# Seven right and nine left expert buffers, row transposes placed behind the up products, mixr beside mixc, and 128-byte operand starts in the second block

## The chip, the cores and the metric

The kernel runs on one core of one Trainium2 chip. Its time is the device time of one execution in microseconds (us); a smaller number is better. Before the change three executions took 3399.05, 3403.66 and 3410.57 us, median 3403.66 us.

## The reference

The kernel computes two transformer-like blocks on 512 tokens of width 2048, all in float32.

The first block normalises x, projects it with w_in, and runs two mixers on the projection: a gated depthwise convolution (31 taps) and a linear-attention scan over 16 heads of 64. Their outputs, 1024 wide each, are joined and go through w_out:

```python
    mixed = jnp.concatenate([y_conv, y_rwkv], axis=-1)
    h = h + mixed @ w_out[l]
    v = rms_norm(h, norm_ffn[l])
    h = h + hierarchical_moe(v, router_group_w[l], ...)
    return rms_norm(h, norm_final)
```

The mixture of experts picks one group of eight by four group logits, then two of that group's eight experts by 32 expert logits; each expert is `silu(x @ w_gate) * (x @ w_up) @ w_down` with a hidden width of 512. There are 32 experts, and all their weights (three matrices of 4 MB each) are read.

The second block normalises, projects to eight parts, and runs sliding-window attention (16 heads of 64 in 4 key groups, window 128) and a diagonal complex state-space recurrence (64 groups, 64 states) side by side:

```python
    q, k, v, a_gate, u, z, g_a, g_s = split(h @ w_in)
    y_a = (attention(q, k, v, sinks) * silu(a_gate)) @ w_attn_proj
    y_ssm = gelu(s5_ssm(u, ...))
    glu_a, glu_b = split(y_ssm @ w_glu + b_glu)
    y_s = (glu_a * sigmoid(glu_b) * silu(z)) @ w_ssm_proj
    merged = sigmoid(g_a) * y_a + sigmoid(g_s) * y_s
    x = x + merged @ w_out
```

## The kernel before, in words

The program has three stages, one after the other in the span: phase A (the first block up to w_out, to about 1017 us), phase B (routing and the experts, to about 2030 us) and phase C (the second block, to the end). A scheduler in the framework orders the instructions of each engine by its own model of their times; a `with tc.issue_after(ins)` block asks that what is issued in it stands behind `ins`. Engines run their instructions in order. Tiles live in pools, on the left or the right side of the on-chip memory; a pool that is closed gives its addresses to the next one, and an instruction that writes there waits for the last reader of the old tile.

**Dense products.** A product in float32 is split into three (`mm3`, L110 to 113): each operand x is held as a rounded part `xh` and a rest `xl`, and the sum is `ah@bh + ah@bl + al@bh`. In the phase C layout the moving operand of a product is an activation tile (128 x 512) and the stationary one a 128 x 128 piece of weights; in w_out of phase A it is the other way round, with weights moving. `weights` (L99) loads a piece by SyncE's queue into `wraw`, ScalarE rounds it (`wh`, L47), VectorE forms the rest (`wl`, L48; GpSimd in w_out(0)). The activations are `uh`/`ul` in phase A, `u2h`/`u2l` for the 16 x 128-row normalised input of the second block, `ge` (the state-space output), `ys` (the gated one), `att` (attention) and `mg` (the merged one).

**w_out in two halves.** `w_out(0)` (L250) multiplies the convolution output `mixc`, `w_out(1)` the scan output `mixr`. `mixr` and the row tiles `xr` come from a right-side pool `mixr`, opened when the pools before it are closed. Behind each quarter of columns of `w_out(1)`, `routed` (L699) transposes the new rows (L708), copies them to `hT` (L711, L713), and adds their part to the router logits: for the first three quarters by four products of 36 x 512 (L717), turned round at the end of the third (L725), for the last by 16 products of 128 x 36 (L731). The rows are also written to memory (`dTok`, L274).

**Experts.** The experts run in 16 pairs, and each pair takes 24 loads of 1 MB on SyncE's queue (L672): gate and up for four quarters of the inner dimension, then down for four quarters of the columns, for both experts. The loads go round 16 buffers, `NW[0]` in the right pool `expw` and `NW[1]` in the left pool `expw2`; the down loads of the last pair go left in any case. Up to `NW[0]` loads are issued during w_out(1) (L258), the next `NW[1]` when the left pool is there. For the rows of a pair there is a gather by an indirect transfer on GpSimd's queue into one tile `xg` (L787), which is set to zero once before (L764); `turned` (L804) transposes `xg` on TensorE (L811). `main` (L903) runs gate and up products (L912), then calls `then`, the transposes for the next pair, then the down products (L933).

**Phase C.** u, k, v and q are projected first. Then the state-space recurrence runs on VectorE, 126 dependent steps (L1297 to L1301) in a pool `ssm2`, with dense products of other projections beside it; the scheduler mixes them. The attention (L1341 to L1371, pool `attn` on the right side) is 16 steps of TensorE, VectorE and ScalarE work. Then come the projections of the gates, w_glu, w_attn and w_ssm, and w_out2.

Of the kernel before, what the change touches and what calls it, by code (L numbers as in the profile page):

```python
# [8 lines left out]
F32 = mybir.dt.float32  # L9
# [3 lines left out]
AF = mybir.ActivationFunctionType  # L13
OP = mybir.AluOpType
AX = mybir.AxisListType
NW = (11, 5)
BREAK = 7
# [3 lines left out]
T = 512  # L21
# [77 lines left out]
def weights(k, src, kts, m, key="w", eng=None):  # L99

    nc = k.nc
    raw = k.wraw.tile([128, kts, m], F32, name=key + "raw")
    k.wload = nc.sync.dma_start(raw, src)
    wh = k.wspl.tile([128, kts, m], F32R, name=key + "h")
    wl = k.wspl.tile([128, kts, m], F32R, name=key + "l")
    split(nc, raw, wh, wl, eng)
    return wh, wl


# [58 lines left out]
def phase_a(k):  # L168
# [81 lines left out]
    def w_out(half, held=None):  # L250

        mh, ml = mix[half]
        for i, n in enumerate((3, 0, 1, 2) if half else range(4)):
            ns = slice(n * 512, (n + 1) * 512)
            ps = held if half and n == 3 else [k.psd.tile([128, T], F32, name="pd") for _ in range(4)]
            for j in range(8):
                wh, wl = weights(k, a["w_out"][half, n, j], 1, 512, eng=None if half else nc.gpsimd)
                if half and (j == 7 or i and j % 2):  # L258
                    with tc.issue_after(k.wload.ins):
                        k.ahead(1, NW[0])  # L260
# [381 lines left out]
    rm = mctx.enter_context(tc.tile_pool(name="mixr", bufs=1, side=RIGHT))  # L642
    k.dH = tc.dram_tile([T, D], F32, name="dTok")
    k.rw = rm.tile([128, KT, 36], F32, name="rw")
    k.lgT = tmp.tile([128, T], F32, name="sg")
    nc.scalar.dma_start(k.rw, a["router_w"])
# [52 lines left out]
def routed(k, psr, tmp, xs, n, i):  # L699

    nc = k.nc
    for t, x in enumerate(xs):
# [6 lines left out]
        else:  # L712
            nc.scalar.activation(ht, pt, AF.Copy)  # L713
    if i < 3:
        pl = psr.tile([128, T], F32, name="pr")
        for j in range(4):
            nc.tensor.matmul(pl[0:36], k.rw[:, 4 * n + j], k.hT[:, 4 * n + j], start=j == 0, stop=j == 3)  # L717
        if i == 0:
            nc.scalar.activation(k.lgT[0:36], pl[0:36], AF.Copy)
        else:  # L720
            nc.vector.tensor_add(k.lgT[0:36], k.lgT[0:36], pl[0:36])
        if i == 2:
            pl = psr.tile([128, 4, 36], F32, name="pr")
            for t in range(4):
                nc.tensor.transpose(pl[:, t], k.lgT[0:36, t * 128:(t + 1) * 128], k.ident[0:36, 0:36])  # L725
            nc.scalar.activation(k.lg, pl, AF.Copy)
    else:
        pl = psr.tile([128, 4, 36], F32, name="pr")
        for t in range(4):
            for j in range(4):  # L730
                nc.tensor.matmul(pl[:, t], k.hT[:, 4 * n + j, t * 128:(t + 1) * 128], k.rw[:, 4 * n + j],  # L731
                                 start=j == 0, stop=j == 3)
        nc.vector.tensor_add(k.lg, k.lg, pl)
    for t, x in enumerate(xs):
# [4 lines left out]
def phase_b(k, upto):  # L739
# [23 lines left out]
    xg = xgp.tile([128, D], F32, name="xg")  # L763
    nc.gpsimd.memset(xg, 0.0)  # L764
    bf = ctx.enter_context(tc.tile_pool(name="b_front", bufs=2, side=LEFT))
# [137 lines left out]
    def main(xT, info, oht, es, load=k.take, then=None, last=None):  # L903
        nq = slice(0, 64 * len(es))
        pgu = [ps0.tile([128, 512], F32, name=n) for n in ("pgate", "pup")]
        for j0 in range(0, KT, 4):
            for wi, which in enumerate(("gate", "up")):
                ws = [load(e, which, j0 // 4) for e in es]
                for j in range(4):
                    for i, w in enumerate(ws):  # L910
                        q = slice(i * 64, (i + 1) * 64)
                        nc.tensor.matmul(pgu[wi][q], xT[:, j0 + j, q], w[:, j * 512:(j + 1) * 512],  # L912
                                         start=j0 + j == 0, stop=j0 + j == KT - 1)
        if then is not None:
            then()
        sl = bf.tile([128, 512], F32, name="sl", bufs=1)
# [59 lines left out]
    def last():  # L976

        k.bctx.close()
        k.uctx = ExitStack()
        up = k.uctx.enter_context(tc.tile_pool(name="u2", bufs=1, side=RIGHT))  # L980
        u = k.u = up.tile([128, KT, T], F32R, name="u2h"), up.tile([128, KT, T], F32R, name="u2l")
# [202 lines left out]
def phase_c(k, out):  # L1184
    nc, tc, a = k.nc, k.tc, k.a
    ctx = ExitStack()
    k.wraw = ctx.enter_context(tc.tile_pool(name="wraw2", bufs=4, side=LEFT))
    k.wspl = ctx.enter_context(tc.tile_pool(name="wspl2", bufs=3, side=LEFT))
# [6 lines left out]
    R1 = c.tile([128, T], F32, name="R1")  # L1195
    R = c.tile([128, T], F32, name="R")

    k.psd = Turns([ctx.enter_context(tc.tile_pool(name="psd%d" % i, bufs=2, space=PSUM)) for i in (2, 3)])
    psr = ctx.enter_context(tc.tile_pool(name="psr2", bufs=3, space=PSUM))
    pss = ctx.enter_context(tc.tile_pool(name="pss2", bufs=1, space=PSUM))  # L1200
    tmp = ctx.enter_context(tc.tile_pool(name="tmp2", bufs=2, side=LEFT))
    u = k.u

    with tc.tile_pool(name="nrm", bufs=2, side=LEFT) as np_:
# [10 lines left out]
        for x, r, e in ((acc[1], R, 1e-12), (acc[0], R1, 1e-6)):  # L1215
            pr = psr.tile([128, T], F32, name="pr")
            nc.tensor.matmul(pr, k.ones, x, start=True, stop=True)
            nc.vector.tensor_scalar(x, pr, 1.0 / D, e, op0=OP.mult, op1=OP.add)
            rsqrt(k, tmp, x, [128, T], r)

# [14 lines left out]
    def qk_norm(x, n, sc):  # L1235
# [4 lines left out]
        nc.vector.tensor_scalar(sq, pn, sc / 64, sc * 1e-6, op0=OP.mult, op1=OP.add)  # L1240
        rs = rsqrt(k, tmp, sq, [128, T])
        nc.vector.scalar_tensor_tensor(x, x, col(k, n), rs, op0=OP.mult, op1=OP.mult)
# [88 lines left out]
    for b in range(4):  # L1331
        bs = slice(b * 128, (b + 1) * 128)
        for g in range(4):
# [40 lines left out]
            nc.sync.dma_start(dO[g, :, :, bs], ot)  # L1374
    actx.close()

    def parked(n, m):
# [42 lines left out]
    k.hctx.close()  # L1420

    yp = ctx2.enter_context(tc.tile_pool(name="ysp", bufs=1, side=RIGHT))
    ys = (yp.tile([128, 8, T], F32R, name="ys_h"), yp.tile([128, 8, T], F32R, name="ys_l"))
# [149 lines left out]
```

## Time and profile before

| what | value |
|---|---|
| median of three executions | 3403.66 us |
| the profiled execution's own time | 3409.05 us |
| its span (first to last instruction) | 3407.4 us |
| TensorE busy | 3187.8 us, 94% |
| VectorE busy | 1654.7 us, 49% |
| ScalarE busy | 1057.3 us, 31% |
| mean granted TensorE clock | 0.966 |
| data moved | 743.47 MB, mean 218 GB/s |

The profile is one execution. Busy time is the time in which an engine had an instruction under way; a TensorE that is shown as busy may still start its matmuls at a wider or narrower distance, so its pace is read from the start times of a run of equal matmuls. In the rows a line is "start, duration, engine, line of the kernel, operation, written tile <- read tiles, shape, count, [idle time before it <- what ended it]". Rows of DMA queues end in q (SPq, POOLq).

### The profile page before, as it was taken

What the parts mean: (1) busy time and instruction counts of PE and PEld (TensorE: products, weight loads), DVE (VectorE), ACT (ScalarE), POOL (GpSimd) and SP (SyncE); (2) the same over time, 40 slices, a digit from 0 to 9 for tenths busy, and PEclk for the clock granted to TensorE, in tenths of its full rate; (3) what the DMA queues carried; (4) which work ended last, traced back from release to release, by engine and by line L of the source; (5) the groups of instructions that cost most, each with busy time, mean ns of one, the idle gap of its engine ahead of it and who ended that gap; (6) DMA issues with size and microseconds to landing.
All of it is one profiled execution on the core that took longest, in us unless ns stands there. A gap on an engine that the chain in (4) does not pass through costs nothing. (4 is left out here: it accounts for less than half of the span.)

```text
span 3407.4 us, 41331 instructions
## 1 busy us (share of the span) xinstructions
PE 3187.8 (94%) x15156; PEld 2172.4 (64%) x15157; DVE 1654.7 (49%) x3072; ACT 1057.3 (31%) x1795; POOL 548.4 (16%) x581
## 2 busy tenths in 40 slices
PE   8999998779998989898999898999999999999999
PEld 6777776647764333343333336778777778888887
DVE  6666667894333223232223248445799443344433
ACT  6464564334330000000000024363322242253322
POOL 3042354543210000000000005272000100000000
PEclk9999999779998999999999999999999999999999
DMA  4545444667668999998999965435332653334443
GB/s 149 131 116 139 119 125 117 133 137 175 220 221 352 419 420 419 411 408 349 420 420 420 411 247 172 145 142 160 133 105 103 194 192 120 121 127 139 133 146 118
DMA packets 352495, 743.47 MB, mean 218 GB/s; under 512 B 110688, under 2 KB 176608, under 8 KB 302112
## 3 DMA queue, kind: packets, MB, share of 16 engines
q1 hardware_dynamic: 272576, 650.24, 52.1%
q10 hardware_dynamic: 70624, 60.52, 7.2%
q0 software_dynamic: 9088, 30.03, 2.7%
q8 instruction: 121, 1.98, 0.2%
q14 instruction: 86, 0.70, 0.1%
HBM read 674.96 MB, written 73.01 MB: 220 GB/s over the span
## 5 line engine op out<-in xcount | busy, mean ns | idle before, releaser
L48 DVE TENSOR_TENSOR wl<-wraw,wh 128x512 fp32r<-128x512 f32 x636 | 477.0, 752 | 498.6 <-ACT wh L47 480.4
L47 ACT ACTIVATE wh<-wraw 128x512 fp32r<-128x512 f32 x668 | 418.6, 630 | 851.1 <-PE pd L112 679.9
L113 PE MATMUL pd<-u2h,wl 128*128 128x512 f32 x1088 | 437.0, 402 | 12.5 <-DVE wl L48 12.5
L111 PE MATMUL pd<-u2h,wh 128*128 128x512 f32 x1088 | 437.6, 402 | 4.7 <-ACT wh L47 4.7
L112 PE MATMUL pd<-u2l,wh 128*128 128x512 f32 x1088 | 433.8, 399 | 0.0
L113 PE MATMUL pd<-uh,wl 128*128 128x512 f32 x688 | 284.5, 414 | 36.5 <-DVE wl L48 36.4
L912 PE MATMUL pgate<-w,xT 128*64 128x512 f32 x1024 | 301.2, 606 | 15.2 <-DMA w<-expert_w_gate_dram 15.2
L912 PE MATMUL pup<-w,xT 128*64 128x512 f32 x1024 | 294.0, 595 | 1.2 <-DMA w<-expert_w_up_dram 1.2
L111 PE MATMUL pd<-uh,wh 128*128 128x512 f32 x688 | 281.6, 410 | 13.3 <-ACT uh L220 7.2
L112 PE MATMUL pd<-ul,wh 128*128 128x512 f32 x688 | 279.3, 406 | 3.9 <-DVE ul L221 3.9
L113 PEld LDWEIGHTS pd<-u2h,wl 128*128 128x128 f32 x1088 | 205.5, 189 | 66.4 <-DVE wl L48 17.5
L309 POOL TENSOR_TENSOR cv<-cv,tap 128x512 f32<-128x512 f32 x150 | 225.8, 1505 | 113.7 <-ACT tap L308 102.2
L111 PEld LDWEIGHTS pd<-u2h,wh 128*128 128x128 f32 x1088 | 205.8, 189 | 54.8 <-ACT wh L47 7.0
L933 PE MATMUL py<-w,hidT 128*64 128x512 f32 x1024 | 235.4, 596 | 3.4 <-ACT hidT L925 2.9
L112 PEld LDWEIGHTS pd<-u2l,wh 128*128 128x128 f32 x1088 | 205.7, 189 | 47.4 <-issue 0.9
L944 DVE TENSOR_TENSOR hT<-hT,pb 128x512 f32<-128x512 f32 x256 | 159.3, 683 | 150.4 <-PE pb L943 150.4
L937 DVE SCALAR_TENSOR_TENSOR yl<-py,info,yh 128x512 fp32r<-128x512 f32 x64 | 48.0, 751 | 304.4 <-ACT yh L936 304.4
L912 PEld LDWEIGHTS pgate<-w,xT 128*64 128x64 f32 x1024 | 86.3, 139 | 166.0 <-issue 147.7
L113 PEld LDWEIGHTS pd<-uh,wl 128*128 128x128 f32 x688 | 135.1, 196 | 77.8 <-DVE wl L48 47.7
L912 PEld LDWEIGHTS pup<-w,xT 128*64 128x64 f32 x1024 | 86.8, 137 | 137.0 <-issue 131.0
L111 PEld LDWEIGHTS pd<-uh,wh 128*128 128x128 f32 x688 | 135.3, 197 | 45.9 <-ACT wh L47 8.9
L933 PEld LDWEIGHTS py<-w,hidT 128*64 128x64 f32 x1024 | 71.7, 137 | 143.9 <-issue 132.3
(566 smaller groups left out, 4981.1 us busy)
## 6 DMA issues: line engine op xcount, KB each, us to landing
w<-expert_w_gate_dram SPq DMA_DIRECT2D x128, 1024.0 KB, 15.2
w<-expert_w_up_dram SPq DMA_DIRECT2D x128, 1024.0 KB, 15.6
w<-expert_w_down_dram SPq DMA_DIRECT2D x128, 1024.0 KB, 14.5
wraw<-w_out_dram SPq DMA_DIRECT2D x128, 256.0 KB, 2.8
wraw<-w_rkv_dram SPq DMA_DIRECT2D x96, 256.0 KB, 3.1
wraw<-w_conv_dram SPq DMA_DIRECT2D x64, 256.0 KB, 3.4
wraw<-w_ga_dram SPq DMA_DIRECT2D x64, 256.0 KB, 2.7
wraw<-w_gs_dram SPq DMA_DIRECT2D x64, 256.0 KB, 2.5
```

Of the source, the lines that this page charges most:

```text
L47: nc.scalar.activation(h, x, AF.Copy)
L48: (eng or nc.vector).tensor_sub(l, x, h)
L111: nc.tensor.matmul(ps, ah, bh, start=first, stop=False)
L112: nc.tensor.matmul(ps, ah, bl, start=False, stop=False)
L113: nc.tensor.matmul(ps, al, bh, start=False, stop=last)
L309: nc.gpsimd.tensor_add(cv[p], cv[p], pr)
L912: nc.tensor.matmul(pgu[wi][q], xT[:, j0 + j, q], w[:, j * 512:(j + 1) * 512], start=j0 + j == 0, stop=j0 + j == KT - 1)
L933: nc.tensor.matmul(py[q], hidT[:, j, q], w[:, j * 512:(j + 1) * 512], start=j == 0, stop=j == 3)
L937: nc.vector.scalar_tensor_tensor(yl[nq], py[nq], info[nq, 0:1], yh[nq], op0=OP.mult, op1=OP.subtract)
L944: nc.vector.tensor_add(hT[:, f], hT[:, f], ps)
```

## The change

Six things are changed, and nothing in what is computed.

1. The 16 expert buffers are split 7 right and 9 left in place of 11 and 5, and the rule by which w_out(1) issues loads ahead is thinned to match (seven in place of eleven).
2. The call of `then` in `main` is put under `issue_after` of the last up product.
3. The pool `mixr` gets its four `xr` tiles first, so that `rw` and the two `mixr` halves lie further up, beside `mixc` (last addresses of `mixc` 97664; `mixr_h` from 101920 in place of 60960).
4. `routed` adds the logits of all four quarters by 16 products of 128 x 36 into `lg`, and the turned tile `lgT` goes.
5. `xg` is filled once by a transfer of 128 rows of x on GpSimd's queue in place of the memset.
6. In phase C pads shift the pools, so that `u2`, `att`, `ge`, `ys` and `mg` start at multiples of 128 bytes. Before they started at 96 (`u2`, `ys`) and 64 (`att`, `ge`, `mg`) past one; `uh` and `mixc` start at a multiple before and after, `mixr` at 32 past one in both. Two scratch tiles of the norm move into a pool of their own (`tn`). With these shifts `attn` lies at 117056 to 127488, and `ssm2`, which reaches to 119424, has to be free before it.

```diff
-NW = (11, 5)
+NW = (7, 9)
...
+def pad(k, ctx, side, n):
+
+    p = ctx.enter_context(k.tc.tile_pool(name="pad", bufs=1, side=side))
+    return p.tile([128, n // 4], F32, name="pad")
...
-                if half and (j == 7 or i and j % 2):
+                if half and (j == 7 or i and j == 3):
...
+    rm.tile([128, 512], F32, name="xr", bufs=4)
     k.rw = rm.tile([128, KT, 36], F32, name="rw")
-    k.lgT = tmp.tile([128, T], F32, name="sg")
...
-    if i < 3:
-        pl = psr.tile([128, T], F32, name="pr")
+    pl = psr.tile([128, 4, 36], F32, name="pr")
+    for t in range(4):
         for j in range(4):
-            nc.tensor.matmul(pl[0:36], k.rw[:, 4 * n + j], k.hT[:, 4 * n + j], start=j == 0, stop=j == 3)
...
+            nc.tensor.matmul(pl[:, t], k.hT[:, 4 * n + j, t * 128:(t + 1) * 128], k.rw[:, 4 * n + j], start=j == 0,
+                             stop=j == 3)
+    if i:
+        nc.vector.tensor_add(k.lg, k.lg, pl)
     else:
...
+        nc.vector.tensor_copy(k.lg, pl)
...
-    nc.gpsimd.memset(xg, 0.0)
+    nc.gpsimd.dma_start(xg, a["x"][0:128])
...
-                        nc.tensor.matmul(pgu[wi][q], xT[:, j0 + j, q], w[:, j * 512:(j + 1) * 512],
+                        up = nc.tensor.matmul(pgu[wi][q], xT[:, j0 + j, q], w[:, j * 512:(j + 1) * 512],
...
         if then is not None:
-            then()
+            with tc.issue_after(up.ins):
+                then()
...
+        pad(k, k.uctx, RIGHT, 3552)
         up = k.uctx.enter_context(tc.tile_pool(name="u2", bufs=1, side=RIGHT))
...
+    pad(k, ctx, LEFT, 128)
     k.wraw = ctx.enter_context(tc.tile_pool(name="wraw2", bufs=4, side=LEFT))
...
+    c.tile([128, 48], F32, name="fill")
...
-            rsqrt(k, tmp, x, [128, T], r)
+            rsqrt(k, tn, x, [128, T], r)
...
+    pad(k, ctx2, RIGHT, 3552)
     yp = ctx2.enter_context(tc.tile_pool(name="ysp", bufs=1, side=RIGHT))
```

Three places show how the order of instructions moves. Line numbers of the changed kernel differ by a few (its L678 is L672 of before, L711 is L708, L117 to L119 are L111 to L113, L720 is L717 and L731, L1295 to L1299 are L1297 to L1301).

On SyncE's queue, in w_out(1) before: one expert load (L672) stands behind every second weight load (L103).

```order
L672 DMA w<-expert_w_gate_dram 128x2048
L103 DMA wraw<-w_out_dram 128x512 x2
L672 DMA w<-expert_w_gate_dram 128x2048
L103 DMA wraw<-w_out_dram 128x512 x2
L672 DMA w<-expert_w_up_dram 128x2048
L103 DMA wraw<-w_out_dram 128x512 x2
```

The same place of the changed kernel, up to the end of w_out(1).

```order
L678 DMA w<-expert_w_gate_dram 128x2048
L103 DMA wraw<-w_out_dram 128x512 x4
L678 DMA w<-expert_w_gate_dram 128x2048
L103 DMA wraw<-w_out_dram 128x512 x4
L678 DMA w<-expert_w_up_dram 128x2048 x2
L678 DMA w<-expert_w_gate_dram 128x2048 x2
L678 DMA w<-expert_w_up_dram 128x2048 x2
```

An expert load now follows every fourth weight load, and the other nine stand behind the last weight load.

On TensorE, behind the first quarter of w_out(1), before: the transposes of the last 128 rows (L708) are followed by dense products of the next quarter; the four logit products (L717) come twenty rows later.

```order
L708 MATMUL pr<-ident,xr 128x128 x4
L111 MATMUL pd<-wh,mixr_h 128x512
L112 MATMUL pd<-wl,mixr_h 128x512
L113 MATMUL pd<-wh,mixr_l 128x512
L111 MATMUL pd<-wh,mixr_h 128x512
L112 MATMUL pd<-wl,mixr_h 128x512
```

The same place of the changed kernel.

```order
L711 MATMUL pr<-ident,xr 128x128 x4
L720 MATMUL pr<-rw,hT 128x36 x12
L117 MATMUL pd<-wh,mixr_h 128x512
L118 MATMUL pd<-wl,mixr_h 128x512
L720 MATMUL pr<-rw,hT 128x36 x4
L119 MATMUL pd<-wh,mixr_l 128x512
```

Twelve (in the second and third quarter four) logit products now stand directly behind the transposes whose copies they read.

On VectorE, in the state-space recurrence before: the four lines of a step (L1297 to L1301) stand between weight rests (L48) and attention work (L1362, L1365).

```order
L1297 TENSOR_TENSOR st_16642<-a_69,S 128x64
L1299 TENSOR_TENSOR st_16643<-a_69,S 128x32 x2
L1300 TENSOR_TENSOR st_16642<-st_16642,st_16643 128x64
L1362 TENSOR_TENSOR PC<-pr,hT 128x512
L1365 TENSOR_TENSOR PP<-pr,hT 128x512
L1301 TENSOR_TENSOR S<-S,st_16642 128x64
L48 TENSOR_TENSOR wl<-wraw,wh 128x512
```

The recurrence in the changed kernel.

```order
L1295 TENSOR_TENSOR st_16691<-a_69,S 128x64
L1297 TENSOR_TENSOR st_16692<-a_69,S 128x32 x2
L48 TENSOR_TENSOR wl<-wraw,wh 128x512
L1298 TENSOR_TENSOR st_16691<-st_16691,st_16692 128x64
L1299 TENSOR_TENSOR S<-S,st_16691 128x64
```

No attention work is left between the steps: all of it stands behind the recurrence, one attention step per 72 dense matmuls. From the first to the last step of the recurrence TensorE's order holds 867 dense matmuls and eleven attention steps before, and 839 dense matmuls and none of attention after. The order of L811 against the up products (L912) is the same before and after in every pair but one, in which the transposes stand one up product later.

## Rows read from the trace of the kernel before

**Rows 1.** Chain that ended last, page section 4: shares of the span by line.
```profile
PE pd L113 10%; PE pd L111 10%; PE pd L112 10%; PE pr L1341 1%; POOL cn L1111 1%; PE ps L1292 0%; POOL cm L1110 0%; DMA yt<-dY 0%; PE pr L1371 0%; DMA kt<-dU 0%; DMA wraw<-w_ga_dram 0%; DMA Ci<-C_im_dram 0%; PE pr L1369 0%; DVE wl L48 0%; PE pr L1239 0%
```

**Rows 2.** Stretch: busy us (instructions) of PE, PEld, DVE, ACT, POOL; clock, DMA share, GB/s.
```profile
1060.00:1360.00 300.00, 276.69 (x1249) 113.85 (x1245) 80.89 (x135) 22.96 (x35) 3.99 (x4) 0.97 1.01 420
...
2424.00:2666.00 242.00, 242.00 (x1157) 187.86 (x1155) 221.09 (x841) 66.07 (x126) 0.00 (x0) 1.00 0.30 105
```

**Rows 3.** Timeline of TensorE, w_in product with uh: first and last of nine matmuls.
```profile
149.73 0.39 PE L112 MATMUL pd<-ul,wh 128*128 128x512 f32 x1
...
151.54 0.39 PE L111 MATMUL pd<-uh,wh 128*128 128x512 f32 x1
```

**Rows 4.** Timeline of TensorE, product with u2h: first and last of 28 matmuls.
```profile
2849.64 0.40 PE L112 MATMUL pd<-u2l,wh 128*128 128x512 f32 x1
...
2855.94 0.40 PE L112 MATMUL pd<-u2l,wh 128*128 128x512 f32 x1
```

**Rows 5.** Timeline of TensorE, w_out(0): first and last of eleven matmuls with mixc.
```profile
870.00 0.39 PE L112 MATMUL pd<-wl,mixc_h 128*128 128x512 f32 x1
...
872.28 0.39 PE L113 MATMUL pd<-wh,mixc_l 128*128 128x512 f32 x1
```

**Rows 6.** Timeline of TensorE, w_out(1): first and last of ten matmuls with mixr.
```profile
990.04 0.39 PE L111 MATMUL pd<-wh,mixr_h 128*128 128x512 f32 x1
...
992.14 0.39 PE L111 MATMUL pd<-wh,mixr_h 128*128 128x512 f32 x1
```

**Rows 7.** Costliest groups, page section 5: the products with u2h, wl.
```profile
L113 PE MATMUL pd<-u2h,wl 128*128 128x512 f32 x1088 | 437.0, 402 | 12.5 <-DVE wl L48 12.5
```

**Rows 8.** By tile, TensorE: durations in ns (min/median/max), first and last start.
```profile
L111 PE MATMUL pd<-ge_h,wh x128: 397/397/398, 2960.0 to 3048.9; 128*128 128x512 f32 x128
L111 PE MATMUL pd<-ys_h,wh x128: 393/396/398, 3055.2 to 3226.6; 128*128 128x512 f32 x128
L111 PE MATMUL pd<-att_h,wh x128: 387/388/398, 3049.6 to 3221.0; 128*128 128x512 f32 x128
L111 PE MATMUL pd<-mg_h,wh x256: 387/388/388, 3227.3 to 3402.4; 128*128 128x512 f32 x128
```

**Rows 9.** Waits of TensorE, 895 to 1060 us: total, times, longest.
```profile
PE pd L111 <- ACT mixr_h L47: 4.7, 3, 2.7
```

**Rows 10.** Timeline of TensorE behind the longest of them: ten slow matmuls.
```profile
915.13 0.63 PE L111 MATMUL pd<-wh,mixr_h 128*128 128x512 f32 x1
...
918.89 0.40 PE L111 MATMUL pd<-wh,mixr_h 128*128 128x512 f32 x1
```

**Rows 11.** Timeline, end of w_out(1): last logit products, memset, start of the routing chain.
```profile
1013.74 3.52 PE L731 MATMUL pr<-rw,hT 128*128 128x36 f32 x30
...
1017.37 1.80 POOL L764 MEMSET xg<- 128x2048 f32 x1 [3.79 <-PE pr L731]
...
1017.71 1.49 DVE L163 TENSOR_SCALAR rstd<-ssqt 128x4 f32<-128x4 f32 x1
```

**Rows 12.** Groups of TensorE, 928 to 1015 us: logit products of three quarters.
```profile
L717 PE MATMUL pr<-hT,rw 128*36 128x512 f32 x24 | 10.9, 596 | 0.0
```

**Rows 13.** Waits of TensorE, 1040 to 2000 us.
```profile
PE pb L811 <- DMA xg<-dTok,ix: 63.7, 11, 7.6
```

**Rows 14.** Recurrence on VectorE, by line: the count of L1301, first and last start.
```profile
L1301 DVE TENSOR_TENSOR S<-S,st x126: 257/274/283, 2422.5 to 2664.2; 128x64 f32<-128x64 f32 x126
```

**Rows 15.** Groups of VectorE, 2424 to 2666 us: what stands between its steps.
```profile
L48 DVE TENSOR_TENSOR wl<-wraw,wh 128x512 fp32r<-128x512 f32 x71 | 48.8, 687 | 3.2 <-ACT wh L47 2.6
...
L1383 DVE TENSOR_TENSOR us<-pd,R 128x512 f32<-128x512 f32 x18 | 12.3, 685 | 1.0 <-PE pd L113 0.6
```

**Rows 16.** Timeline of VectorE: starts of three steps, one weight rest before the third.
```profile
2502.99 0.28 DVE L1297 TENSOR_TENSOR st<-a,S 128x64 f32<-128x64 f32 x1
...
2504.13 0.28 DVE L1297 TENSOR_TENSOR st<-a,S 128x64 f32<-128x64 f32 x1
...
2505.74 0.28 DVE L1297 TENSOR_TENSOR st<-a,S 128x64 f32<-128x64 f32 x1
```

More of the change, by code (lines that the diff above doesn't have):

```diff
@@ L713, in routed @@
             nc.scalar.activation(ht, pt, AF.Copy)
-    if i < 3:
-        pl = psr.tile([128, T], F32, name="pr")
+    pl = psr.tile([128, 4, 36], F32, name="pr")
+    for t in range(4):
         for j in range(4):
-            nc.tensor.matmul(pl[0:36], k.rw[:, 4 * n + j], k.hT[:, 4 * n + j], start=j == 0, stop=j == 3)
[L718 to L726, printed above, removed]
-    else:
[L728 to L733, printed above, removed]
+            nc.tensor.matmul(pl[:, t], k.hT[:, 4 * n + j, t * 128:(t + 1) * 128], k.rw[:, 4 * n + j], start=j == 0,
+                             stop=j == 3)
+    if i:
+        nc.vector.tensor_add(k.lg, k.lg, pl)
+    else:
+        nc.vector.tensor_copy(k.lg, pl)
     for t, x in enumerate(xs):
@@ L1201, in phase_c @@
     tmp = ctx.enter_context(tc.tile_pool(name="tmp2", bufs=2, side=LEFT))
+    nctx = ExitStack()
+    tn = nctx.enter_context(tc.tile_pool(name="tn", bufs=1, side=LEFT))
     u = k.u
@@ L1240, in qk_norm @@
         nc.vector.tensor_scalar(sq, pn, sc / 64, sc * 1e-6, op0=OP.mult, op1=OP.add)
-        rs = rsqrt(k, tmp, sq, [128, T])
+        rs = rsqrt(k, tn, sq, [128, T])
         nc.vector.scalar_tensor_tensor(x, x, col(k, n), rs, op0=OP.mult, op1=OP.mult)
@@ L1375, in phase_c @@
     actx.close()
+    nctx.close()
     def parked(n, m):
```

## The prediction

> **What bounds the kernel now.** I read the chain of waits first. The reader is to see that its largest lines are the three dense matmuls of the split product, L111 to L113, 10% of the span each, and that nothing else on it holds more than 1% [rows 1]. So a change is worth what it does to the pace of these matmuls, or to a place where TensorE stands still. Busy time by stretch is the second view. It shows two regimes. Among the experts the DMA share is 1.01 at 420 GB/s while TensorE is busy for 276.69 of 300 us: transfers set the pace there, and work taken off TensorE comes back as a longer wait for weights [rows 2]. In the recurrence of phase C TensorE is busy for 242.00 of 242.00 us with a full clock and VectorE for 221.09: TensorE bounds it, with VectorE close behind [rows 2]. "Busy" hides the pace, so the third view is the timeline: the distance from the start of one dense matmul to the next, in runs without a wait. The matmuls all have the same form (128 x 512 moving, 128 x 128 stationary, full clock), and yet there are two paces:
> - uh, which starts at a multiple of 128 bytes: (151.54 - 149.73) / 8 = 0.2263 us [rows 3]
> - u2h, 96 past one: (2855.94 - 2849.64) / 27 = 0.2333 us [rows 4]
> - mixc, at a multiple: (872.28 - 870.00) / 10 = 0.2280 us [rows 5]
> - mixr, 32 past one: (992.14 - 990.04) / 9 = 0.2333 us [rows 6]
>
> mixc and mixr are the same loop of the same code, 120 us apart, with weights from the same pool; they differ by 0.0053 us a matmul. This is the best evidence that the start of an operand in its 128 bytes costs time.
>
> **The change part by part**, against the profiled execution's own time, 3409.05 us. That is 5.4 us above the median of 3403.66; I carry the sum over to the median.
>
> *Aligned operands in phase C.* Aligned pace: the mean of 0.2263 and 0.2280, 0.2271 us. There are three times 1088 matmuls on u2 [rows 7], 3264, and 3264 x (0.2333 - 0.2271) = 20.2 us. ge and ys have 3 x 128 each, 768 together, and their durations are 397 and 396 ns [rows 8], those of the slow pace (0.40 in rows 4): 768 x 0.0062 = 4.8 us. att and mg, 3 x 128 and 3 x 256 = 1152 matmuls, show 388 ns on L111 [rows 8], that of the quick pace (0.39 in rows 3), though they start at 64; I count a third of the difference, 0.002, 2.3 us. Sum 27.3 us, all on TensorE, which the chain names. Ends: nothing at one side (rival A), and 0.2333 - 0.2263 for all of u2, ge and ys with half of it for att and mg at the other, 22.8 + 5.4 + 4.0 = 32 us. A loss has nothing for it: no aligned run is slower than an unaligned one. I stay near the middle, since four runs of matmuls agree.
>
> *Attention behind the recurrence.* The same instructions, moved. Cover is lost: 241.7 us for 126 steps before [rows 14], of which the attention's TensorE work filled part; now 839 dense matmuls have to, 839 x 0.2271 = 190.5 us. VectorE needs, in the same time, 126 bare steps of 2504.13 - 2502.99 = 1.14 us [rows 16], 143.6 us, and in between a weight rest for every 12 matmuls and a scaled result for every 48, 70 + 17 = 87 (71 and 18 before [rows 15]). One of them lengthens a step by 2505.74 - 2504.13 - 1.14 = 0.47 us [rows 16], at most by its whole duration, 0.69 [rows 15]: 41 to 60 us. VectorE's sum is 185 to 204 us against 190.5, so TensorE is to wait -6 to +13 us for the last step or, on the way, for a weight rest that stands behind steps on VectorE's queue. Below zero there is no gain, as TensorE is full. I take +4. The attention's chain itself then has the projections of the gates and all of w_glu beside it, so I add nothing for it; if that cover failed, the products on att would be late.
>
> *mixr beside mixc.* Its splits no longer wait for the last readers of mixc. TensorE waited 4.7 us for mixr_h in three waits [rows 9], and behind the longest ten matmuls ran slow, 918.89 - 915.13 = 3.76 us in place of 10 x 0.2333 [rows 10]: 1.4 us. That is 6.1 us at most, nothing at least (the scan's rows still have to arrive by ScalarE's queue). I take -5.5. mixr keeps its pace, as it still starts 32 past a multiple.
>
> *Logits by 16 small products.* A quarter costs 10.9 / 3 = 3.6 us before [rows 12]; the last quarter, already in the new form, 3.52 us for 30 of its 32 records [rows 11], 3.75. Equal. But the products now stand directly behind the transposes, and wait for the copies in between. Ends: nothing, or three times the longest wait of this half, 2.7 us [rows 9], 8 us. A copy takes about as long as another pass over 128 x 512, 0.69 us [rows 15]: 3 x 0.5 = +1.5, as some is covered.
>
> *Fill of xg by a transfer.* The memset (1.80 us) and the VectorE instruction beside it (1.49 us for 128 x 4 elements) stand at the head of the routing chain, in which TensorE is idle [rows 11]. The transfer can go out when mixr is read for the last time, before the logits. Between 0 and -1.8; I take -1.3.
>
> *Seven and nine buffers.* The ring has 16 either way, so the middle of the experts is as before: 0, with +-6 for transfers that fall otherwise. At the start nine loads in place of five are sent when w_out(1) is done: 9 x 1.0486 MB / 420 GB/s = 22.5 us instead of 12.5. The first gather, which TensorE waits for, then shares the queues with them for longer: 0 to +10, and +1 since five loads were under way beside it before, too. At the end, the last pair's down loads find nine left buffers: 0.
>
> *Transposes held behind up products.* They stood there already in all pairs but one. TensorE waits 63.7 us for xg at this line [rows 13], and goes on to: 0, and in a stretch that transfers bound nothing would be gained anyway.
>
> Sum: -27.3 + 4 - 5.5 + 1.5 - 1.3 + 1 = -27.6 us. 3409.05 - 27.6 = 3381.4 for an execution like the profiled one, 3403.66 - 27.6 = 3376 us for the median.
>
> **Rivals.**
> A. *The address is not the cause.* Against my reading: ge and mg start at the same 64 bytes past a multiple, yet show 397 and 388 ns [rows 8], so a rule by 128 bytes alone isn't the whole of it; the pace may hang on something else, such as what runs beside. Then the 27.3 us fall away, and with matmuls at 0.2333 (195.7 us for 839) the recurrence's wait shrinks to 0: -5.5 + 1.5 - 1.3 + 1 = -4.3, 3399 us. For it speaks the Trainium skill, "SBUF — State Buffer": its section "Operand start alignment" asks of an operand's start no more than a multiple of the element size, for legality and with nothing timed, and by "Who interferes with whom" TensorE's reads never wait on anyone. That leaves no room for the gap between rows 5 and 6, which the trace nonetheless shows.
> B. *VectorE takes over the recurrence.* With 204 us against 190.5 the wait is 13 us, and a clock that falls in the pauses adds some: half the gain of phase C is gone, -27.6 + 9 + 3 = -16, 3388 us. For it: 221.09 of 242 us [rows 2]; against it: VectorE loses all of the attention's work there.
> C. *Slower: the experts' stream starts late.* If the first gather lands only behind all nine loads, TensorE begins the experts 10 us later; and four loads that no longer came during w_out(1) set the transfer-bound stretch back by another 4 x 2.5 = 10 us. With A, -4.3 - 1 + 20 = +15, 3418 us. It decides from the point where the first gate product starts later by more than what alignment gives back; with the gain of 27 us it would only make 3395. For it: DMA share 1.01; against it: the old kernel's queue also stood idle before the experts.
> That the hold does nothing is in the sum already.
>
> **How the numbers follow.** Forecast 0.62 (own range 3364 to 3386), B 0.18, A 0.13, C without alignment 0.05, the rest 0.02. The smallest difference that a measurement of this kernel can tell is about 0.3%, 10 us. Faster by more: forecast, B and a little of the rest, 0.82; within: A, 0.13; slower: 0.05. Range 3360 (alignment at its upper end, no wait) to 3397 (short of A), about 8 in 10.
>
> **What would show it.** Dense matmuls on u2h at a distance of 0.226 to 0.228 us, ge and ys at 388 ns; if they stay at 0.233 and 397, A holds. A wait of TensorE for S or wl of some us at the end of the recurrence, over 10 in case of B. No wait for mixr_h around 899 to 915. The first L912 within 3 us of its old place behind the end of w_out(1); later by 10 or more would be C. The experts' stretch as long as before to 6 us. I am wrong if phase C is not shorter by 15 us or more.

## The result: slower, 3453 us

The changed kernel takes 3453.01 us (median of four executions, 3450.57 to 3458.17) against 3403.48 for the kernel before: a ratio of 1.014, with an interval from 1.0125 to 1.0155. Forecast were 3376 us and a gain; it lost 50 us. The profiled execution has a span of 3450.3 us against 3407.4, 42.9 above; the profiled execution of the kernel before was 5.6 us over its median, this one 1.0 us under its own, which makes up the rest.

**Where the time went.** The busy time by stretch comes first, because it finds the place. The four stretches of the changed kernel are the recurrence, the rest of the products on u2, the gap behind them, and the products on ge (columns: start and end, length, busy us and instructions of TensorE, its weight loads, VectorE, ScalarE, GpSimd, then TensorE's clock, DMA share, GB/s).

```profile
2424.00:2616.00 192.00, 192.00 (x833) 155.85 (x832) 175.25 (x706) 43.32 (x69) 0.00 (x0) 1.00 0.34 120
2616.00:2938.00 322.00, 319.40 (x1579) 254.36 (x1578) 143.11 (x269) 89.86 (x167) 13.30 (x18) 0.99 0.39 130
2938.00:2986.00 48.00, 24.67 (x98) 15.75 (x96) 19.21 (x41) 7.75 (x19) 0.00 (x0) 0.57 0.12 38
2986.00:3100.00 114.00, 100.35 (x406) 79.28 (x407) 56.68 (x85) 75.64 (x105) 0.00 (x0) 0.91 0.47 153
```

The recurrence itself is fine: TensorE is busy all the time, as it was before [rows 2], and the recurrence's last step starts at 2610.4 instead of 2664.2 [rows 14], 188 us behind its first at 2422.2. Then come 48 us in which no engine is busy for more than about half and the granted clock is 0.57, and 114 us with waits. What runs there is told by the tiles. These are the first and last starts, in the changed kernel, of the products on u2, of the attention's second product (one of its last instructions in each step), and of the products on ge (columns: durations min/median/max in ns, then first and last start).

```profile
L117 PE MATMUL pd<-u2h,wh x1088: 387/393/797, 2043.8 to 2938.2; 128*128 128x512 f32 x182
...
L1367 PE MATMUL pr<-PC,hT x64: 379/430/687, 2699.5 to 2981.1; 128*64 128x256 f32 x64
...
L117 PE MATMUL pd<-ge_h,wh x128: 389/389/796, 2985.9 to 3094.5; 128*128 128x512 f32 x128
```

The same rows of the kernel before are these, with one more behind them that is used further down.

```profile
L1369 PE MATMUL pr<-PC,hT x64: 379/404/431, 2349.9 to 2667.1; 128*64 128x256 f32 x64
...
L111 PE MATMUL pd<-u2h,wh x1088: 389/396/792, 2045.3 to 2959.3; 128*128 128x512 f32 x182
...
L111 PE MATMUL pd<-wh,mixr_h x128: 392/394/628, 899.2 to 1011.2; 128*128 128x512 f32 x128
```

Before, attention ran from 2349.9 to 2667.1, beside the recurrence, and the products on ge (first start 2960.0 [rows 8]) followed those on u2 at once. After, attention starts 350 us later and ends at 2981.1, when the u2 products have been over for 43 us. What holds its start shows on ScalarE: the attention's first write of its tile P (L1341) waits for the transfer that carries off the last tile yb of the recurrence's pool ssm2.

```profile
2678.44 0.60 ACT L1311 ACTIVATE yb<-ps 128x512 f32<-128x512 f32 x1 [3.44 <-PE ps L1310]
...
2682.48 0.66 ACT L1341 ACTIVATE P<-pr 128x256 f32<-128x256 f32 x2 [2.02 <-DMA dY<-yb]
```

The timeline of TensorE in that gap shows how it then goes (the brackets give the idle time before and what ended it).

```profile
2949.66 1.09 PE L1358 MATMUL pr<-ident,P 128*128 128x128 f32 x4 [6.84 <-DVE P L1355]
...
2963.89 1.09 PE L1358 MATMUL pr<-ident,P 128*128 128x128 f32 x4 [5.27 <-DVE P L1355]
...
2978.12 1.09 PE L1358 MATMUL pr<-ident,P 128*128 128x128 f32 x4 [5.27 <-DVE P L1355]
...
2985.89 1.22 PE L117 MATMUL pd<-ge_h,wh 128*128 128x512 f32 x2 [3.33 <-ACT ge_h L47]
```

The last three attention steps run bare, one every 14.2 us, each a chain from TensorE to ScalarE to VectorE and back with nothing beside it. Earlier steps had products on u2 beside them, one step per 72 dense matmuls, as the order in "The change" has it. From 2682.48 on, 925 matmuls on u2 were left, and 16 steps of 72 want 1152: they sufficed for 13 steps. Why couldn't w_glu's products fill the gap? ScalarE's timeline answers: the function that makes the input of ge (L1407) ran twice, at 2630.8 and 2638.6, but the first rounding of ge (L47) waits until the attention's last output has been written out.

```profile
2638.59 1.16 ACT L1407 ACTIVATE sq<-yt 128x512 f32<-128x512 f32 x1 [2.61 <-DVE yt L1405]
...
2982.65 0.38 ACT L1371 ACTIVATE ot<-pr 128x256 f32<-128x256 f32 x1 [6.53 <-PE pr L1369]
2985.21 1.15 ACT L47 ACTIVATE ge_h<-sq 128x512 fp32r<-128x512 f32 x2 [2.17 <-DMA dO<-ot]
```

The addresses explain both waits (bytes in a partition, from the layout of the kernel's pools; a trace does not show them). ge_l lies at 109952 to 126336, attn at 117056 to 127488. So there were two waits by address: attention waits for ssm2 (up to 119424), and ge waits for attention. The second existed before, too (113728 to 130112 against 120608 to 131040), but attention was over 290 us before TensorE wanted ge. What TensorE then waited for most from 2940 to 3110 us (total, times, longest):

```profile
PE pr L1358 <- DVE P L1355: 17.4, 3, 6.8
PE pd L117 <- ACT wh L47: 11.3, 3, 8.7
PE pd L117 <- ACT ge_h L47: 4.2, 3, 3.3
PE pr L1367 <- DVE PC L1360: 2.6, 3, 0.9
```

The sum of it: the products on ge start 2985.9 - 2960.0 = 25.9 us later, and take 3094.5 - 2985.9 = 108.6 us from the first start to the last, 19.7 more than 3048.9 - 2960.0 [rows 8], with these waits and matmuls of up to 796 ns where there were none over 398. ScalarE has 75.64 of these 114 us to do, as it now forms ge and att here, and rounds the weights (wh) in the same queue. That is 46 us by the end of ge; att, ys and mg give 3 back. The 25.9 us are a net sum: the products on u2 end 21.1 us sooner than before (2938.2 against 2959.3), in part since three attention steps no longer stand among them.

**The pace.** The second surprise of the profile after is that u2 hardly got quicker. Two starts nine matmuls apart:

```profile
2849.68 0.39 PE L117 MATMUL pd<-u2h,wh 128*128 128x512 f32 x1
...
2851.77 0.40 PE L117 MATMUL pd<-u2h,wh 128*128 128x512 f32 x1
```

That is 2.09 / 9 = 0.2322 us, though u2h now starts at a multiple of 128 (before 0.2333 [rows 4]). ys stayed slow, too, while ge fell from 397 to 389 ns, where mg (388 before [rows 8]) is as well:

```profile
L117 PE MATMUL pd<-ys_h,wh x128: 392/394/399, 3100.6 to 3271.2; 128*128 128x512 f32 x128
...
L117 PE MATMUL pd<-mg_h,wh x256: 389/389/393, 3271.9 to 3445.3; 128*128 128x512 f32 x128
```

The starts tell them apart: u2h 127488 and ys_h 193024 are even multiples of 128, ge_h and mg_h 93568 and att_h 60800 odd ones, as are the weights of phase C (27776). The quick ones stand at the same place as their weights within 256 bytes (that is, modulo 256), the slow ones 128 away.

**The beginning.** From 885 to 1075 us the waits of the changed kernel are:

```profile
PE pb L803 <- DMA xg<-dTok,ix: 8.1, 1, 8.1
...
PE pd L117 <- ACT mixr_h L47: 4.4, 3, 1.8
```

The wait for mixr_h did not go (4.7 before [rows 9]), and the first gather, which brings the rows of the first pair of experts, is waited for 8.1 us (3.6 before; the row stands at "The buffers alone").

### The profile page after: what moved, and what is told of

It is laid out like the page before. It is cut to its first block, busy times and chain, and to the rows that moved or that the text cites. A ratio compares the mean times of both kernels' runs of the same rounds, so it can differ in the third digit from the quotient of the medians.

```text
span 3450.3 us, 41494 instructions
## 1 busy us (share of the span) xinstructions
PE 3197.6 (93%) x15224; PEld 2193.3 (64%) x15225; DVE 1664.7 (48%) x3073; ACT 1056.6 (31%) x1794; POOL 545.0 (16%) x581
## 4 chain that ended last, share of the span: by engine, by line
PE 47%; DMA 4%; DVE 2%; POOL 1%; ACT 1%; issue 1%; ACTq 0%; SPq 0%; DVEq 0%; POOLq 0%
PE pd L117 11%; PE pd L119 11%; PE pd L118 11%; PE py L926 3%; PE pgate L904 3%; PE pup L904 3%; DMA w<-expert_w_gate_dram 1%; DMA xg<-dTok,ix 1%; PE pb L935 1%; PE pb L936 1%; PE pr L1339 1%; DMA w<-expert_w_up_dram 1%; PE pb L803 0%; PE ps L1290 0%; PE pr L1369 0%
## 5 line engine op out<-in xcount | busy, mean ns | idle before, releaser
L48 DVE TENSOR_TENSOR wl<-wraw,wh 128x512 fp32r<-128x512 f32 x636 | 476.7, 752 | 427.4 <-ACT wh L47 418.7
L47 ACT ACTIVATE wh<-wraw 128x512 fp32r<-128x512 f32 x668 | 418.2, 629 | 837.7 <-PE pd L118 661.5
L119 PE MATMUL pd<-u2h,wl 128*128 128x512 f32 x1088 | 434.7, 399 | 10.4 <-DVE wl L48 10.4
L117 PE MATMUL pd<-u2h,wh 128*128 128x512 f32 x1088 | 437.0, 402 | 4.8 <-ACT wh L47 4.8
L119 PE MATMUL pd<-uh,wl 128*128 128x512 f32 x688 | 284.8, 414 | 36.9 <-DVE wl L48 36.8
L117 PE MATMUL pd<-uh,wh 128*128 128x512 f32 x688 | 281.0, 409 | 11.9 <-ACT uh L226 7.3
L119 PEld LDWEIGHTS pd<-u2h,wl 128*128 128x128 f32 x1088 | 205.8, 189 | 60.5 <-DVE wl L48 13.2
L117 PEld LDWEIGHTS pd<-u2h,wh 128*128 128x128 f32 x1088 | 206.0, 189 | 53.9 <-ACT wh L47 6.1
L119 PEld LDWEIGHTS pd<-uh,wl 128*128 128x128 f32 x688 | 135.2, 196 | 77.4 <-DVE wl L48 47.2
L117 PEld LDWEIGHTS pd<-uh,wh 128*128 128x128 f32 x688 | 135.8, 197 | 44.4 <-ACT uh L226 7.0
```

What stands on the lines that cost most here:

```text
L47: nc.scalar.activation(h, x, AF.Copy)
L48: (eng or nc.vector).tensor_sub(l, x, h)
L117: nc.tensor.matmul(ps, ah, bh, start=first, stop=False)
L119: nc.tensor.matmul(ps, al, bh, start=False, stop=last)
```

## The experiments

Theory 1 was that the pad of 3552 bytes caused the loss by its place: it moved attn into ssm2. The rival was that one of the other parts did. A second question was what sets the pace. Ratios are to runs of the kernel before on the same chip (medians 3407.78 to 3408.5).

**A smaller pad.** 96 bytes also bring u2 and ys to multiples of 128, odd ones this time, and leave attn at 120512, clear of ssm2.

```diff
-        pad(k, k.uctx, RIGHT, 3552)
+        pad(k, k.uctx, RIGHT, 96)
...
-    pad(k, ctx2, RIGHT, 3552)
+    pad(k, ctx2, RIGHT, 96)
```

> The changed kernel with both right-side pads of phase C cut from 3552 to 96 bytes: u2h starts at 130944, ys_h at 196480 (both odd multiples of 128), attn at 120512, clear of ssm2, which ends at 119424. Theory 1 (the loss is attention that had to wait for ssm2, then ran bare, with ge behind it): attention goes back between the steps of the recurrence, no wait for P before L1358 near the end of the u2 products, time 3370 to 3395 us. Within it: if the pace follows whether an operand starts at an odd multiple of 128, u2 and ys fall from 0.2326 to 0.227 us a matmul and the time is about 3372; if u2 stays at 0.2326 whatever its start, about 3393. Rival (the loss comes from another part, such as the nine late loads or the logits): still over 3435.

Measured: 3389.85 us, ratio 0.9952 (0.994 to 0.9965). Attention is back beside the recurrence (its second product runs from 2346.2 to 2657.9), and there is no gap behind u2. The pace of u2 in this kernel:

```profile
2849.71 0.39 PE L118 MATMUL pd<-u2l,wh 128*128 128x512 f32 x1
...
2853.79 0.39 PE L118 MATMUL pd<-u2l,wh 128*128 128x512 f32 x1
```

4.08 / 18 = 0.2267 us. So the loss goes with the pads' size, and an odd multiple gives u2 the quick pace. The time is still 18 us above the 3372 expected for it; 4 of them are the chip's (the kernel before took 3407.78 there), and the other parts don't pay (below).

**The move alone.** The kernel before, with attn moved down by 3584 bytes and all starts kept in their place modulo 512.

```diff
+        pad(k, k.uctx, RIGHT, 3584)
         up = k.uctx.enter_context(tc.tile_pool(name="u2", bufs=1, side=RIGHT))
...
+    nctx = ExitStack()
+    tn = nctx.enter_context(tc.tile_pool(name="tn", bufs=1, side=LEFT))
...
-            rsqrt(k, tmp, x, [128, T], r)
+            rsqrt(k, tn, x, [128, T], r)
...
```

> The kernel before with its attn pool moved down by 3584 bytes (a pad ahead of u2, the norm's scratch in a pool of its own to make room) and nothing else: attn at 117024 overlaps ssm2, all starts of operands keep their place within 512 bytes, so their paces stay as before. Theory 1: 3440 to 3460 us, with the last attention steps bare behind the u2 products as in the changed kernel, that is, the whole loss. Rival: about 3403, since nothing that the rival blames is in it.

Measured: 3458.68 us, ratio 1.0155 (1.013 to 1.0179), 51 us over the kernel before (44 to 61 by the interval). Its attention runs from 2698.0 to 2980.5, and its waits from 2900 to 3110 us are those of the changed kernel (L1369 is L1358 there):

```profile
PE pr L1369 <- DVE P L1366: 17.7, 3, 7.1
PE pd L117 <- ACT wh L47: 11.6, 3, 9.2
PE pd L117 <- ACT ge_h L47: 4.2, 3, 3.4
```

The whole loss is in this one edit.

**Nearly the same move without the overlap.** The kernel before with the pool tn for the norm's scratch as in the run above, a pad of 3072 bytes and one yb buffer in place of two, so that ssm2 ends at 117056 and attn starts at 117536.

```diff
+        pad(k, k.uctx, RIGHT, 3072)
...
-        yb = s2.tile([128, 4, NCH], F32, name="yb")
+        yb = s2.tile([128, 4, NCH], F32, name="yb", bufs=1)
...
```

> The kernel before with attn moved down by 3072 bytes and one yb buffer in place of two, so that ssm2 ends at 117056 and attn (117536) is clear of it. Theory 1: attention stands between the steps of the recurrence again, 3400 to 3412 us, although attn has moved nearly as far as in the run that lost 51 us. Rival (the move itself, or the pool for the norm's scratch, costs the time): 3440 or more.

Measured: 3409.11 us, ratio 1.0004 (0.9993 to 1.0014). The row of the attention's second product (here L1378) is back at its old place:

```profile
L1378 PE MATMUL pr<-PC,hT x64: 379/404/431, 2344.3 to 2661.5; 128*64 128x256 f32 x64
```

So it is neither the move nor the pool for the norm's scratch, but the overlap, which in the run above was about 2 KB, one buffer of ssm2.

**Weights moved by 128 bytes.** As the kernel with pads of 96, with the weights of phase C at even multiples and every activation left at its odd one.

```diff
-    pad(k, ctx, LEFT, 128)
+    pad(k, ctx, LEFT, 256)
...
-    c.tile([128, 48], F32, name="fill")
+    c.tile([128, 16], F32, name="fill")
```

> As the kernel with pads of 96 bytes, but the weight tiles of phase C start 128 bytes further up (27904 in place of 27776, an even multiple of 128), all activations as there (odd multiples). If the pace is set by the distance of the two operands within 256 bytes, then u2, ge, att, ys and mg all run at 0.2325 us a matmul and the time is some 30 us over the kernel with pads of 96. If it is set by the activation's own start, they run at 0.227 and the time is the same within 5 us.

Measured: 3412.69 us, ratio 1.0014 (1.0001 to 1.0027), 23 us more than with pads of 96. Its products on mg, first and last of 13:

```profile
3299.71 0.40 PE L119 MATMUL pd<-mg_h,wl 128*128 128x512 f32 x1
...
3302.51 0.40 PE L119 MATMUL pd<-mg_h,wl 128*128 128x512 f32 x1
```

2.80 / 12 = 0.2333 us, with mg where it ran at 0.2267. It is the distance of the two operands that counts, not the start of either. The 30 us expected were somewhat many: 23, with an interval of 4 us to either side on each of the two times. That the pace went as expected is told by the starts, not by the time.

**Parts 1 to 5 without phase C.** Buffers 7 and 9, hold, mixr, logits and the fill of xg, with phase C as before.

```diff
-NW = (11, 5)
+NW = (7, 9)
...
```

> Parts 1 to 5 of the change (buffers 7 and 9, held transposes, mixr beside mixc, small logit products, fill of xg by a transfer) with phase C as before. Theory 1: 3394 to 3404 us, a gain of 0 to 9 of mixr less what the later gather costs. Rival: 3435 or more, as the loss lies in these parts.

Measured: 3414.35 us, ratio 1.0012 (0.9998 to 1.0026). That is over the 3394 to 3404 expected: no gain, if anything a loss of some 4 us by the ratio. Against it the alignment of phase C, done right, is worth 3414.35 - 3389.85 = 24.5 us.

**Old buffers and old mixr, with pads of 96** (parts 1 and 3 undone).

```diff
-NW = (7, 9)
+NW = (11, 5)
...
-    rm.tile([128, 512], F32, name="xr", bufs=4)
```

> The kernel with pads of 96 bytes, with the eleven and five buffers and the old place of mixr again (parts 1 and 3 undone). Theory: the nine late loads cost the first gather 4.4 us (TensorE waited 8.1 us for xg at 1036 us in place of 3.6) and mixr beside mixc gave nothing, as ScalarE forms mixr_h in its queue's order, behind the last weight pieces of w_out(0). Expected: 3 to 5 us less than with pads of 96 alone (ratio to the kernel before about 0.994), the wait for the first gather back under 5 us, the waits for mixr_h the same 4.5 us. Rival (mixr beside mixc did save its 5 us, hidden by other losses): as much or more than with pads of 96.

Measured: 3390.28 us, ratio 0.9944 (0.993 to 0.9958); the difference to pads of 96 alone is within the intervals. So the 3 to 5 us expected do not show in the time. The trace is clearer: xg is waited for 5.4 us, a little over the 5 expected, and mixr_h 5.0.

```profile
PE pb L802 <- DMA xg<-dTok,ix: 5.4, 1, 5.4
PE pd L117 <- ACT mixr_h L47: 5.0, 3, 2.2
```

**The buffers alone**, on the kernel before.

```diff
-NW = (11, 5)
+NW = (7, 9)
...
-                if half and (j == 7 or i and j % 2):
+                if half and (j == 7 or i and j == 3):
```

> The kernel before with seven right and nine left buffers and the thinned rule, and nothing else. Theory: the first gather lands later, TensorE waits 8 us for it in place of 3.6, time 3 to 6 us over the kernel before (ratio 1.001 to 1.002). Rival (the gather is late for the transfer that fills xg, which goes out on the same queue just ahead of it): no change, wait 3.6 us.

Measured: 3409.99 us, ratio 1.000 (0.999 to 1.001): the expected 3 to 6 us did not show in the time, though 3 of them would lie within the interval. In the trace the gather is late as expected (the kernel before first, then this run):

```profile
PE pb L811 <- DMA xg<-dTok,ix: 3.6, 1, 3.6
...
PE pb L811 <- DMA xg<-dTok,ix: 8.0, 1, 8.0
```

That is 8.0 against 3.6 us in the kernel before, so the nine loads lengthen the wait for the first gather by 4.4 us, and the transfer that fills xg (absent here, present above with 5.4) by some 1.8. The two don't add up: with both the wait is 8.1.

**mixr at the place of its weights** (on the kernel with old buffers).

```diff
+    rm.tile([128, 40], F32, name="fill")
     for p in range(8):
```

> The same with mixr moved by 160 bytes, so that it starts at the same place within 256 bytes (128) as the weights of phase A. If the distance of the two operands within 256 bytes sets the pace, the matmuls on mixr go from 0.233 to 0.227 or 0.228 us, 384 x 0.0055 = 2 us less. If it is something that mixr alone has (its time, the transfers beside it), they stay at 0.233.

Measured: 3387.42 us, ratio 0.9937 (0.9924 to 0.9951). Seven matmuls on mixr:

```profile
959.78 0.39 PE L119 MATMUL pd<-wh,mixr_l 128*128 128x512 f32 x1
...
961.14 0.39 PE L119 MATMUL pd<-wh,mixr_l 128*128 128x512 f32 x1
```

1.36 / 6 = 0.2267 us against 0.2333 [rows 6]. The distance explains mixr, too. That the time fell by 3 us is within the intervals.

**xr in a pool of its own** (on the kernel with pads of 96). In the changed kernel rw and the first mixr_h stand on ScalarE's queue like this:

```profile
893.11 0.34 ACTq L652 DMA_DIRECT2D rw<-router_w_dram  x1
893.50 0.63 ACT L47 ACTIVATE mixr_h<-sq 128x512 fp32r<-128x512 f32 x1 [2.42 <-PE pd L119]
```

rw waits for the last matmul of w_out(0) though its own addresses are free: the pool it is in reaches from 91424, and its lowest 6 KB, xr, lie in mixc.

```diff
-    rm.tile([128, 512], F32, name="xr", bufs=4)
...
+    rx = mctx.enter_context(tc.tile_pool(name="mixx", bufs=1, side=RIGHT))
...
-                xr = (rm if half else cm).tile([128, 512], F32, name="xr", bufs=4)
+                xr = (rx if half else cm).tile([128, 512], F32, name="xr", bufs=4)
```

> The kernel with pads of 96 bytes, with the xr tiles in a pool of their own, so that the pool of rw and mixr (99616 and up) is wholly clear of mixc (up to 97664). Theory: in the changed kernel mixr_h still waited 4.4 us because the pool as a whole, xr tiles included, reached down to 91424 into mixc, and the first transfer into it, rw, waits on ScalarE's queue for the last matmul of w_out(0), with the splits of mixr behind it. Now rw waits for no TensorE instruction and four of the eight splits come before the end of w_out(0): waits for mixr_h under 1.5 us in all, the part from the first to the last mixr matmul 3 to 5 us shorter than 109.7, time 3384 to 3388 (ratio 0.993 to 0.995). Rival (the rows of the scan arrive late in any case): waits for mixr_h stay at 4 us and more.

Measured: 3389.72 us, ratio 0.9953 (0.994 to 0.9966), the same as without. But the wait is gone: rw goes out at 885.7 in place of 893.1 us with the first splits behind it, the end of w_out(0) is within 1 us of its place, and none of the waits from 885 to 1075 us is for mixr_h any more.

```profile
885.69 0.34 ACTq L651 DMA_DIRECT2D rw<-router_w_dram  x1
886.08 1.15 ACT L47 ACTIVATE mixr_h<-sq 128x512 fp32r<-128x512 f32 x2 [2.18 <-DMA dYr<-y]
```

So the mechanism is as expected. Its worth was not: the matmuls on mixr span 107.9 us (893.9 to 1001.8) in place of 109.7, where 104.7 to 106.7 were expected, and 2 us are below what the executions scatter by.

**All that helps** (the same, with mixr at the place of its weights).

```diff
+    rm.tile([128, 40], F32, name="fill")
     rx = mctx.enter_context(tc.tile_pool(name="mixx", bufs=1, side=RIGHT))
```

> The same with 160 bytes left free, so that mixr starts at the place of the phase A weights within 256 bytes: 2 us less again (ratio about 0.993), mixr matmuls at 0.227 to 0.228 us. It still has the nine late loads, which cost the first gather some 4 us (TensorE waits 8 us for xg).

Measured: 3379.7 us, ratio 0.9928 (0.9915 to 0.9941). This is the quickest version, 2% under the changed kernel and 0.7% under the kernel before. It is 10 us under the run above, where 2 were expected. The trace accounts for about 4 of them: the matmuls on mixr span 103.6 us (893.2 to 996.8) instead of 107.9. Where the others come from is not shown.

## Why the prediction was wrong, step by step

- *Attention behind the recurrence* is the step that failed. It allowed +4 us for a VectorE that might become too slow, and then: "The attention's chain itself then has the projections of the gates and all of w_glu beside it, so I add nothing for it". The first half was right: TensorE stayed busy through the recurrence, which took 188 us where 185 to 204 were forecast for VectorE, and the waits from 2616 to 2938 us sum to under 3 us. The second half was not. w_glu was no cover, because ge waits for attn's addresses; and the projections of the gates were used up before the attention's last steps, 925 matmuls where 16 steps in that order want 1152. The prediction did name the case that the cover fails, but it gave it no price, and saw the products on att late, not those on ge. The loss was 51 us, shown by the move alone. As an estimate, the order has a share in it: 16 steps at the bare 14.2 us are 227 us, and the u2 products went on for 256 us behind 2682.5, so steps that stand closer might have ended with them; this was not tried. The overlap of attn and ssm2 had been read from the addresses; that of ge and attn is nowhere in the prediction. It costs nothing as long as attention comes early.
- *Aligned operands*: the term was -27.3. Done with the distance right, it is worth 24.5 (pads of 96 against parts 1 to 5 alone, with some 6 us of interval to either side), so the size held. In the changed kernel only ge, att and mg got it, and u2 a tenth of it. From the mean distance of starts over each whole stream that is an estimated 3264 x 0.0006 on u2, 384 x 0.006 on ge and 1152 x 0.002 on att and mg, 7 us in all. The rule was wrong: "a multiple of 128" where the runs show "the same place as the other operand within 256 bytes". Rows 3 to 6 could not tell these apart: uh and mixc stand at 0 from their weights by that count, u2h and mixr don't. Rival A was right that 128 bytes were not the whole of it, and wrong that the address is not the cause. By the Trainium skill, "SBUF — State Buffer", section "Who interferes with whom", TensorE never waits on anyone. By these runs a matmul takes 0.0066 us longer (0.2333 against 0.2267) when its two operands start 128 bytes apart modulo 256; whether one of its reads then waits for the other, they don't show.
- *mixr beside mixc*: -5.5 forecast, nothing measured (4.4 us of waits in place of 4.7). A pool waits as a whole, and one load ahead in ScalarE's queue passed the wait on.
- *Logits*: +1.5 forecast for waits. The matmuls of w_out(1) span 112.0 us before (899.2 to 1011.2, row above), and 109.7 with only the logits changed there (old buffers and mixr, row below), with the same waits for mixr_h.

```profile
L117 PE MATMUL pd<-wh,mixr_h x128: 388/394/500, 895.6 to 1005.3; 128*128 128x512 f32 x128
```

In the other traces with mixr's pace and waits unchanged it is 111.1 to 112.8 us with the old logits and 109.1 to 111.1 with the new ones. So they gave about 2 us and cost none; which instruction gave them was not followed up.
- *Fill of xg*: -1.3 forecast. TensorE's wait before the routing fell from 8.6 us to 7.8 (rows below: before, then the changed kernel), and with nine late loads the gather behind it was waited for 8.1 us with the transfer and 8.0 without: about -0.7 in the changed kernel. Beside the old buffers the gather's wait grew by 1.8, and the sum was about +1.

```profile
PE pb L865 <- DVE M L859: 8.6, 1, 8.6
...
PE pb L857 <- DVE M L851: 7.8, 1, 7.8
```

- *Seven and nine buffers*: +1 forecast, with 10 as the upper end; the wait for the gather rose by 4.4 us. The time of the run with this part alone rose by 1.5 us, within its interval.
- *Hold*: forecast was nothing. It was not tried alone, because TensorE's order did not change but in one pair; so that it does nothing is argued from this, not shown.

What the runs show adds up: +51 for the overlap, +4 for parts 1 to 5 by the ratio, -7 by the estimate for the alignment, 48 us against the 49.5 measured.

The range reached to 3397 and left out a slower outcome but for 5 in 100. The rival on that side (C) looked at the experts, where little happened: the first gate product came 3.7 us later behind the end of w_out(1) than before. It did not look at the one step that gave up 240 us of cover. Rival B fell, as TensorE was busy for 192.00 of 192.00 us in the recurrence.

## What to carry to other kernels

A pad is not free of time: before you shift a pool, list for both sides whom it newly overlaps and who has to end first, and follow the chain on (here ssm2, then attention, then ge) up to the next work that TensorE could do. A tile moved off an overlap gains nothing while its pool as a whole, or an instruction ahead of it in its queue, still waits. Operands of a matmul are best compared with each other: keep moving and stationary tile at the same place within 256 bytes. This was tried for dense float32 matmuls of one form alone.

## What was not expected of the hardware

The distance from one dense matmul to the next (128 x 512 moving in float32, full clock) follows how far apart the two operands start, taken modulo 256 bytes: 0.226 to 0.228 us at distance 0 (uh, mixc; ge, att and mg of the changed kernel; all of phase C with pads of 96; mixr where moved), 0.232 to 0.234 at 128 (u2 and ys of the changed kernel, all of phase C with moved weights), 0.233 to 0.234 at 224 (u2 and ys of the kernel before) and at 160 (mixr there). Other distances were not tried but 64, and why it is so is not shown. At distance 64 it is not settled: in the kernel before ge ran at 397 ns and att at 388 [rows 8] (0.2333 and 0.229 us from start to start), and in the kernel with only the buffers changed, with all of phase C at the same addresses, ge ran like att:

```profile
L111 PE MATMUL pd<-ge_h,wh x128: 388/388/388, 2963.2 to 3050.4; 128*128 128x512 f32 x128
L113 PE MATMUL pd<-ge_h,wl x128: 394/394/394, 2963.7 to 3050.9; 128*128 128x512 f32 x128
```

In the run of parts 1 to 5, at the same addresses once more, ge ran at 0.2333 again. So at 64 something besides the addresses decides, and what it is stays open.
